# Turning the output projection and both feed-forward stages of a hybrid attention layer so that features lie on the partitions

## The chip, the cores and the metric

One core of a Trainium2 chip runs the whole layer in one program. Its engines have their own instruction streams: PE (matrix products, with PEld loading the stationary operand), DVE and POOL (both elementwise; POOL is GpSimd), ACT (activations, casts, copies), and SP, which issues most of the transfers (DMA). The metric is the device time of one execution in microseconds (us); less is better.

## The reference

The layer works on 1024 tokens with 1024 features, in float32:

```python
u = rms_norm(h, mix_norm_gain);  proj = u @ w_in
o_att = rms_norm(chunked_rel_attention(aq, ak, av, ...), att_out_gain)   # 8 heads of 64, band of 9 chunks
o_dn  = rms_norm(gated_delta_rule(dq, dk, dv, ...), dn_out_gain) * silu(dgate)   # 4 heads of 128
h = h + concat([o_att, o_dn]) @ w_out
z = rms_norm(h, ffn_norm_gain) @ w_ff1            # 1024 x 1024 by 1024 x 4096
h = h + square(relu(z)) @ w_ff2                   # 1024 x 4096 by 4096 x 1024
```

The change concerns the last three lines: the output projection with its residual, the norm behind it, and the two feed-forward products.

## The kernel before

**Arithmetic.** A float32 operand x is split into hi, which is x rounded to the type that PE multiplies fast (fp32r), and lo = x - hi. A product is then three matmuls: hi by hi, hi by lo, lo by hi. `split` (L130 to L137) does it with a cast on ACT (L134) and a subtraction on DVE or POOL (L137); names that end in `_h` and `_l`, or `h` and `l`, are such halves.

**Stages.** First the norm and all projections from u, then attention and the delta rule interleaved, then `out_proj` (PE tile `op`, L962 and following), `ff1` (tile `q`, L1095) and `ff2` (tile `p`, L1205). The order of the instructions on every engine is set by a scheduler that plans with a timeline of its own, under the limits that pools of buffers set: a tile gets a buffer only when the tile that held it has been read for the last time. No engine reorders at run time.

**Attention and delta rule.** Names with `t_` are one attention turn of 128 tokens (the last three of its steps: normalise the heads' outputs `t_on`, take them through POOL's reciprocal root `t_r`, transpose them into `t_tpo` on PE). Names with `c_` and `m_` are one chunk of the delta rule (`c_po` output, `c_o` its normalised form, `c_tpo` its transpose).

**Output projection.** Tokens lie on the partitions. For each half j of the output columns and each block t of 128 tokens, 24 matmuls multiply the block of mixer outputs with the weights `wo`; DVE adds the residual (L977) into `h`. When a block's both halves are done, its row norm follows: squares on ACT and DVE (L175), root on POOL, scaling (L182), and 8 transposes on PE (`v_tp`, L195; 64 in all), since ff1 wants features on the partitions. DVE and ACT write the transposed blocks with the gain into `b11`, `b21` (first 512 tokens) and `b12`, `b22` (last 512). The norm of the last two blocks is put behind the first two products of ff1 (`rest`).

**ff1.** A Strassen-Winograd scheme with 7 products instead of 8: the columns of w_ff1 are taken in 8 blocks of 512, and each block has products q1, q2, q5, q6, q3, q7, q4 of 24 matmuls each (1344 in all). The operands on the side of u (`b11`, `t1` to `t4`, ...) are made once; the weight sums `ws` are made in every block. Every second lo goes to POOL, the others to DVE; results go to the scratch tensor `f_dr`.

**ff2.** The same scheme over 4 groups of the inner dimension, 7 products of 48 matmuls in each (again 1344). Here both operands of every product are split anew, 512 columns at a time; every third lo goes to POOL, and POOL makes some of the sums (L1276, L1285, L1294). DVE adds the products into the accumulators (L1266); residual pages `r` come back from `h_dr`. In the very last product the matmuls are ordered by output bank ("turned"), so that the four banks end one after another.

All tiles are pages of 512 columns out of pools shared by all stages; PSUM is divided into four pools of 3, 2, 1 and 2 banks.

## Time and profile before

| | us |
|---|---|
| median of 3 runs (lowest, highest) | 1326.9 (1321.51, 1328.15) |
| the profiled execution: own time | 1324.08 |
| the profiled execution: span from first to last instruction | 1322.4 |
| PE busy in it | 1271.4 |
| DVE, POOL, ACT busy in it | 973.2, 717.3, 538.6 |

Rows of the profile are read like this. A row of groups or of the timeline names engine, line and operation, then output <- inputs with shapes; in a group the three numbers behind "xN:" are the shortest, median and longest duration in ns, and first and last start in us. In the view of stretches each engine has its busy us and, in brackets, how many instructions began there; PEclk is the TensorE clock granted, as a share of full speed; then come the share of time the DMA engines were busy and GB/s. Consecutive matmuls overlap, so a matmul listed with 0.39 us can follow another after 0.23 us: PE's rate is read from counts or from starts, not from durations.

### The profile page before, as it was taken

The numbers are of one execution on the slowest core, as the hardware profiler recorded it, in microseconds if no ns is written. First come the engines' busy times: TensorE is split into PE (matmuls) and PEld (weight loads), VectorE is DVE, ScalarE is ACT, GpSimd is POOL, SyncE is SP. The second block draws the span as 40 slices with busy tenths as digits, with TensorE's granted clock in tenths as the row PEclk, the third lists the DMA queues.
The fourth block names the chain that finished last, engine by engine and source line by source line (L and its number), as shares of the span: only waits on it lengthen the run. The fifth ranks groups of instructions, "written<-read, shape, count | busy, mean of one in ns | idle before, by whom it ended". The sixth has DMA issues, their size and how long they took to land.

```text
span 1322.4 us, 19653 instructions
## 1 busy us (share of the span) xinstructions
PE 1271.4 (96%) x6718; PEld 1042.8 (79%) x6718; DVE 973.2 (74%) x1627; ACT 538.6 (41%) x1128; POOL 717.3 (54%) x826
## 2 busy tenths in 40 slices
PE   8999999999999899999988999999997999989997
PEld 6778878788888788888866788888876887867776
DVE  7899969554156567764789966545569799998799
ACT  7232222222266566643653333333314544434331
POOL 4426542543124454651487766554488395683885
PEclk9999999999999999999988999999998999999999
DMA  7214354666564432163403333333581523314002
GB/s 217 69 44 142 95 156 119 151 168 165 191 199 147 135 92 73 38 210 96 128 18 126 109 116 118 112 112 128 195 299 40 166 83 113 119 56 129 31 33 96
DMA packets 133861, 159.71 MB, mean 121 GB/s; under 512 B 25216, under 2 KB 74368, under 8 KB 133760
## 3 DMA queue, kind: packets, MB, share of 16 engines
q1 hardware_dynamic: 125056, 154.25, 37.5%
q10 hardware_dynamic: 8704, 4.20, 1.4%
q8 instruction: 53, 0.87, 0.3%
q14 instruction: 48, 0.39, 0.1%
HBM read 111.22 MB, written 47.19 MB: 120 GB/s over the span
## 4 chain that ended last, share of the span: by engine, by line
PE 62%; DVE 17%; issue 7%; POOL 6%; DMA 4%; ACT 2%; SPq 0%; DVEq 0%; POOLq 0%; ACTq 0%
PE q L1095 18%; PE p L1205 6%; PE op L155 6%; PE av_ps L155 3%; PE aq_ps L155 3%; PE t_o L893 3%; PE g_ps L155 3%; PE ak_ps L155 2%; PE dq_ps L155 2%; PE dv_ps L155 2%; DVE r L1266 1%; POOL b L1276 1%; DVE s L1280 1%; PE t_tpa L883 1%; PE t_tpb L872 1%
## 5 line engine op out<-in xcount | busy, mean ns | idle before, releaser
L1102 POOL TENSOR_TENSOR z<-z 128x512 f32<-128x512 f32 x32 | 42.9, 1341 | 54.0 <-ACT z L1101 39.0
L836 DVE CUSTOM_DVE_ANT_0 t_pb<-t_sb,biasn 128x256 f32<-128x256 f32 (+1 forms) x64 | 25.7, 403 | 54.5 <-PE t_sb L821 29.1
L155 PE MATMUL op<-wo_l,op_h 128*128 128x512 f32 x128 | 50.5, 394 | 0.0
L155 PE MATMUL op<-wo_h,op_h 128*128 128x512 f32 x128 | 49.7, 392 | 0.8 <-DVE h L977 0.8
L155 PE MATMUL op<-wo_h,op_l 128*128 128x512 f32 x128 | 50.1, 392 | 0.0
L1101 ACT ACTIVATE z<-z 128x512 f32<-128x512 f32 x32 | 20.3, 633 | 53.0 <-DVE z L1154 19.9
L1266 DVE TENSOR_TENSOR r<-r,p 128x512 f32<-128x512 f32 x64 | 40.6, 675 | 0.0
L851 ACT ACTIVATE t_pb<-t_pb,t_nm 128x256 f32<-128x256 f32 (+1 forms) x64 | 31.6, 494 | 21.3 <-DVE t_nm L845 12.3
L1122 POOL TENSOR_TENSOR wa<-wa,wa 128x512 f32<-128x512 f32 x16 | 25.5, 1595 | 23.0 <-DVE ws L1109 23.0
L1109 DVE TENSOR_TENSOR ws<-wa,wa 128x512 f32<-128x512 f32 x16 | 16.1, 1007 | 25.9 <-DMA wa<-in_w_ff_dram 25.8
L1276 POOL TENSOR_TENSOR b<-b,b 128x512 f32<-128x512 f32 x16 | 24.6, 1539 | 18.1 <-DVE p13b_l L137 8.7
L1280 DVE TENSOR_TENSOR s<-s,a 128x512 f32<-128x512 f32 x16 | 24.7, 1544 | 10.0 <-POOL p53a_l L137 6.2
L1114 DVE TENSOR_TENSOR ws<-ws,wa 128x512 f32<-128x512 f32 x16 | 18.1, 1132 | 18.0 <-POOL q_3a_l L137 6.2
L845 DVE CUSTOM_DVE_ANT_0 t_pa<-t_sa,biaso,t_nm 128x384 f32<-128x384 f32 (+2 forms) x48 | 26.3, 548 | 5.2 <-PE t_sa L821 2.9
L1294 POOL TENSOR_TENSOR b<-b,b 128x512 f32<-128x512 f32 x16 | 25.9, 1621 | 7.8 <-DVE p21b_l L137 2.5
L1285 POOL TENSOR_TENSOR b<-b,b 128x512 f32<-128x512 f32 x16 | 26.8, 1686 | 5.1 <-DVE p50b_l L137 1.9
L178 POOL TENSOR_TENSOR v_st<-v_ss 128x1 f32<-128x1 f32 x8 | 2.8, 347 | 48.7 <-DVE v_ss L175 48.7
L155 PEld LDWEIGHTS op<-wo_h,op_h 128*128 128x128 f32 x128 | 24.0, 188 | 6.0 <-ACT op_h L134 1.2
L1104 DVE SCALAR_TENSOR_TENSOR z<-z 128x512 f32<-128x512 f32 x32 | 28.6, 893 | 0.0
L893 PE MATMUL t_o<-t_ta,vt 128*64 128x128 f32 x240 | 27.8, 287 | 0.5 <-DVE t_ta L886 0.3
L1274 DVE TENSOR_TENSOR s<-a,a 128x512 f32<-128x512 f32 x16 | 13.1, 824 | 20.5 <-DMA a<-f_dr 15.5
L155 PEld LDWEIGHTS op<-wo_l,op_h 128*128 128x128 f32 x128 | 24.0, 188 | 4.9 <-issue 0.2
(1271 smaller groups left out, 4904.2 us busy)
## 6 DMA issues: line engine op xcount, KB each, us to landing
wa<-in_w_ff_dram SPq DMA_DIRECT2D x64, 256.0 KB
f_dr<-z SPq DMA_DIRECT2D x64, 256.0 KB
a<-f_dr SPq DMA_DIRECT2D x64, 256.0 KB
b<-in_w_ff_dram SPq DMA_DIRECT2D x64, 256.0 KB
t_q<-q_dr SPq DMA_DIRECT2D x32, 256.0 KB
xt<-in_x_t_dram SPq DMA_DIRECT2D x16, 256.0 KB
ks<-k_dr SPq DMA_DIRECT2D x16, 256.0 KB
wo_r<-in_w_out_dram SPq DMA_DIRECT2D x16, 256.0 KB
```

The source lines that it names most:

```text
L155: nc.tensor.matmul(ps, a, b, start=(i == 0), stop=(i == n - 1))
L845: nc.vector.tensor_tensor_reduce(sa[e][:, 0:wa], bk[:, 0:wa], old[g][i][:, 384 - wa:384], -1.0, nm[:, 4 + i:5 + i], ALU.add, ALU.min, nm[: ...
L851: nc.scalar.activation(sb[:, c], sb[:, c], AF.Exp, bias=m, scale=-1.0, accum_out=T["sums"][:, 4 + i:5 + i])
L893: nc.tensor.matmul(po[64 * e:64 * e + 64, pp * P:(pp + 1) * P], vt[k0 + j][:, 64 * h:64 * h + 64], (ta[e] if j < na else tb)[:, c:c + P], ...
L1095: nc.tensor.matmul(ps[q], l[:, s], r, start=(i + k + m == 0), stop=(i + k == 2 and m == 2))
L1102: nc.gpsimd.tensor_tensor(t, t, t, ALU.mult)
L1104: nc.vector.scalar_tensor_tensor(t, t, 0.0, t, ALU.max, ALU.mult)
L1205: nc.tensor.matmul(ps[q], l[:, s], r, start=(i == 0 and m == 0), stop=(i == NK - 1 and m == 2))
L1266: nc.vector.tensor_tensor(y[q], y[q], ps[q], op)
L1276: nc.gpsimd.tensor_tensor(b11[i], b12[i], b11[i], ALU.subtract)
L1280: nc.vector.tensor_tensor(s1[i], s1[i], a11[i], ALU.subtract)
L1285: nc.gpsimd.tensor_tensor(b11[i], b22[i], b11[i], ALU.subtract)
```

## The change

- The output projection computes its transpose: weights are the stationary operand, the mixer outputs (stored transposed, four blocks to a tile of 2048 columns) the moving one. `rows` makes a quarter h[j, hf] (512 features, 512 tokens) in four banks; the residual comes from the transposed input `x_t`.
- The norm needs a sum over features, which now lie on partitions: ACT squares, POOL adds the squares up (L955 of the new kernel), matmuls with a column of ones (`hcol`) and with a broadcast of the scales (`hrow`) make a row of factors, and DVE scales 16 pages (L965). The 64 transposes and the row norm are gone. The norm of the second half of the tokens, formerly behind the first products of ff1, now stands ahead of them.
- A pool `quarters` of six tiles of 2048 columns holds in turn k^T, half of u's lo parts, the mixer outputs and their normalised forms, the four quarters of h, and ff1's and ff2's results.
- The mixer's pools are closed after the output projection. ff1 and ff2 get pools of their own with pages of 1024 columns and PSUM in four tiles of 1024 columns. Elementwise operations are half as many and twice as wide. POOL keeps the lo parts of b21 and b22, one subtraction and four merges at the end; in ff1 the second half of relu(z)^2 is squared by ACT.
- ff2 multiplies the transposed weights with f, so results are transposed too, and the host returns a transposed view of the output. The last product is no longer turned.
- The raw input pages use 8 buffers in place of 16.

```diff
     def row_scales(squares, hf, name, col, row):      # was row_scales(hf); now also for the second norm
...
         if c % TPH == 0:
+            mix[c // TPH][1] = quarter(f"mixd{c // TPH}")
...
+            if t % TPH == 0:
+                mix[t // TPH][0] = quarter(f"mixa{t // TPH}")
...
     def out_proj():
+        order = (4, 5, 6, 7, 0, 1, 2, 3)
...
+        def rows(j, hf, acc):
+            R[j, hf] = r = quarter(f"h{j}{hf}")
+            for i in range(4):
...
+                mm3(ps, [((w[j][k][0][:, s], w[j][k][1][:, s]), parts[hf][k]) for k in order])
+                nc.vector.tensor_tensor(part(r, i), ps, xt, ALU.add)
+                if i == 0 and acc is None:
+                    acc = page("on", n + "_q")
+                    nc.scalar.activation(acc, part(r, i), AF.Square)
+                else:
+                    sq = page("raw", n + "_q", w=516)[:, 0:512]
+                    nc.scalar.activation(sq, part(r, i), AF.Square)
+                    nc.gpsimd.tensor_tensor(acc, acc, sq, ALU.add)
+            nc.sync.dma_start(out=h_dr[j, hf], in_=q4(r))
+            return acc
+        def norm(hf, acc, js):
+            row = page("pp", f"hr{hf}")
+            row_scales([acc], hf, "h", r_col[:, TPH * hf:TPH * hf + TPH], row)
+            for j in js:
+                for i in range(4):
+                    r = part(R[j, hf], i)
+                    nc.vector.scalar_tensor_tensor(r, r, fgain[:, 4 * j + i:4 * j + i + 1], row, ALU.mult, ALU.mult)
+        weights(0)
+        mixed(0)
+        acc = rows(0, 0, None)
+        weights(1)
+        acc = rows(1, 0, acc)
+        norm(0, acc, (0, 1))
+        mixed(1)
+        acc = rows(1, 1, None)
+        acc = rows(0, 1, acc)
+        norm(1, acc, (0, 1))
+        return dict(b11=R[0, 0], b21=R[1, 0], b12=R[0, 1], b22=R[1, 1])
...
     def ff1(R, psw, pools):
...
+                split(t, hi, lo, nc.scalar, nc.gpsimd if key in ("b21", "b22") else nc.vector)
...
+            z11 = wide(zz, 0) if zz is not None else page2("ut4", f"z11_{sb}")
...
+            z12 = wide(zz, 1) if zz is not None else page2("ut4", f"z12_{sb}")
...
         def product(name, prep):                       # ff2
+            ps = [psw.tile([P, 1024], F32, tag="bk", name=f"{name}{m}") for m in range(2)]
+            for i in range(2):
+                ab = []
+                for o, src in zip("ab", prep(i)):
+                    hi = page2("h" + t, f"{name}{o}{i}_h", F32R)
+                    lo = page2("l" + t, f"{name}{o}{i}_l", F32R)
+                    split(src, hi, lo, nc.scalar, nc.vector)
...
-    ff1(*out_proj())
-    ff2()
+    R = out_proj()
+    mixer.close()
+    ffn(R)
```

The order of the instructions moves at four places. The rows that follow are the order on one engine, with the line number of the respective kernel.

**PE at the end of attention.** Before: `t_on` and `t_tpo` are the last turns, `op` the output projection, `c_po` the delta rule.

```order
L155 MATMUL op_6683<-wo_7_h,op_h_6684 128x512
L155 MATMUL op_6720<-wo_7_h,op_h_6721 128x512
L913 MATMUL t_on<-ident,t_pb_6518 128x128 x2
L502 MATMUL t_tpo<-ident,t_on 128x128 x4
L155 MATMUL op_6683<-wo_7_l,op_h_6684 128x512
L155 MATMUL op_6683<-wo_7_h,op_l_6685 128x512
L155 MATMUL op_6683<-wo_0_h,op_h_6688 128x512
```

After:

```order
L852 MATMUL t_o<-t_tb_6560,vt_3775 64x128 x2
L852 MATMUL t_o<-t_tb_6560,vt_3778 64x128 x2
L874 MATMUL t_on<-ident,t_pb_6500 128x128 x2
L460 MATMUL t_tpo<-ident,t_on 128x128 x8
L167 MATMUL op_6700<-ml_6666,wo_4_h 128x512
L167 MATMUL op_6700<-mh_6665,wo_4_l 128x512
L167 MATMUL op_6700<-mh_6669,wo_5_h 128x512
```

Before, 35 matmuls of the output projection (and a chunk's `c_po`) stand between the last turn's `t_on` and its transposes; now none does, and the transposes of the last two turns stand together. Only three `op` matmuls stand ahead of this place.

**DVE, first attention turns.** After, the rows that free the banks of the first two turns' transposes (`mixa<-t_tpo`, in one row) stand behind the fifth chunk's `mixd`; before, the corresponding L928 of the first two turns stood each in its turn's place, ahead of the fourth chunk's L717.

```order
L606 TENSOR_TENSOR c_jv<-c_tpv,br 128x512
L481 TENSOR_REDUCE c5q_ss<-c_tpq 128x4
L612 SCALAR_TENSOR_TENSOR c_jv<-c_pk,nbr,c_jv 128x128 x4
L676 SCALAR_TENSOR_TENSOR mixd_5069<-c_tpo,dng,c_jg 128x4x128
L891 TENSOR_TENSOR mixa_5825<-t_tpo,again 128x4x128 x2
```

Two banks (`ps_t`) serve the transposes of attention, so both are held until then.

**DVE from the last output bank to the first products of ff1**, after (`hcol` comes from PE, `hr` from ACT):

```order
L948 TENSOR_TENSOR h_7181<-op_7277,op_x 128x512
L129 TENSOR_SCALAR h_v<-hcol_7308 128x4
L134 TENSOR_TENSOR h_t<-h_y 128x4
L136 SCALAR_TENSOR_TENSOR h_t<-h_t,h_v 128x4
L137 SCALAR_TENSOR_TENSOR r_col<-h_t,h_y 128x4
L965 SCALAR_TENSOR_TENSOR h_7181<-h_7181,fgain,hr_7307 128x512 x4
L965 SCALAR_TENSOR_TENSOR h_7056<-h_7056,fgain,hr_7307 128x512 x4
L149 TENSOR_TENSOR b11l_7362<-h_6697,b11h_7361 128x1024
L1013 TENSOR_TENSOR h_6697<-h_7181,h_6697 128x1024
L1013 TENSOR_TENSOR h_7181<-h_7056,h_7181 128x1024
L149 TENSOR_TENSOR b11l_7366<-h_6697,b11h_7365 128x1024
L149 TENSOR_TENSOR q_0a_l<-wa_0_7351,q_0a_h 128x1024
```

PE has no other matmul between the norm's `hrow` and ff1's first product. Before, the splits of `b11` and `b21` stood ahead of the last two blocks' norms.

**SP at the end of ff1**, after:

```order
L1055 DMA f_dr<-zz_9144 128x2x512 x2
L1114 DMA y_9325<-h_dr 128x1024 x2
L1055 DMA f_dr<-yy_9084 128x2x512
L1055 DMA f_dr<-z_1_7819 128x2x512
L1151 DMA a_0_9339<-in_w_ff_dram 128x2x512
L1151 DMA a_0_9341<-in_w_ff_dram 128x2x512
L1151 DMA b_0_9343<-f_dr 128x2x512
L1151 DMA b_0_9345<-f_dr 128x2x512
```

`z_1_7819` is the page z12 of ff1's block 1; it takes a buffer of the tag `ut4`, which an operand of the last product of block 7 holds until that product ends. Its store now stands ahead of every load of ff2. Before, ff2's first loads stood among the last stores of ff1.

More of the change, by code (lines that the diff above doesn't have):

```diff
@@ L906, in finish @@
             if not g:
-                outs[t] = page("at", n + "_on")
+                if t % TPH == 0:
+                    on = quarter(n + "_on")
+                    outs.update((t + i, part(on, i)) for i in range(TPH))
             o = outs[t]
@@ L1229, in ff2, with store @@
+        def store(x, j, hf):
+            for m in range(2):
+                nc.sync.dma_start(out=out[0, (4 * j + 2 * m) * P:(4 * j + 2 * m + 2) * P, hf * TH:(hf + 1) * TH].rearrange(
+                    "(q p) t -> p q t", p=P), in_=two(x[m]))
         nb = DFF // (2 * NK * P)
```

632 lines of the change are left out of this document (255 added, 377 removed).

## The prediction

> **What bounds the kernel now.** I read the page first, for who is busy.
>
> ```profile
> PE 1271.4 (96%) x6718; PEld 1042.8 (79%) x6718; DVE 973.2 (74%) x1627; ACT 538.6 (41%) x1128; POOL 717.3 (54%) x826
> PE 62%; DVE 17%; issue 7%; POOL 6%; DMA 4%; ACT 2%; SPq 0%; DVEq 0%; POOLq 0%; ACTq 0%
> ```
>
> PE is the bound, and the chain that ended last runs through it; DVE's 17% and POOL's 6% of that chain are what an edit of the elementwise work can reach. Where they lie is told by the view of stretches around the two feed-forward stages.
>
> ```profile
> core 0: us, PE busy (x) PEld busy (x) DVE busy (x) ACT busy (x) POOL busy (x), PEclk, DMA share, GB/s
> 655.00:670.00 15.00, 14.79 (x73) 11.94 (x72) 9.34 (x19) 7.46 (x16) 9.52 (x15) 1.00 0.20 66
> 670.00:700.00 30.00, 22.35 (x87) 17.10 (x85) 27.62 (x32) 15.62 (x34) 26.48 (x13) 0.88 0.13 39
> 700.00:740.00 40.00, 38.16 (x153) 30.65 (x154) 39.01 (x43) 15.63 (x28) 28.86 (x21) 0.92 0.37 124
> 740.00:780.00 40.00, 40.00 (x178) 33.00 (x177) 25.69 (x32) 13.42 (x24) 28.00 (x20) 1.00 0.36 117
> 940.00:970.00 30.00, 30.00 (x134) 24.82 (x133) 13.52 (x20) 10.73 (x19) 17.84 (x14) 1.00 0.92 325
> 980.00:1010.00 30.00, 24.90 (x96) 19.32 (x95) 24.88 (x22) 11.29 (x21) 21.93 (x15) 0.89 0.35 121
> 1010.00:1050.00 40.00, 37.41 (x165) 30.30 (x164) 35.72 (x42) 17.81 (x32) 21.45 (x15) 1.00 0.39 124
> 1050.00:1100.00 50.00, 49.58 (x218) 40.53 (x217) 45.18 (x42) 21.87 (x40) 41.07 (x26) 1.00 0.23 75
> 1100.00:1150.00 50.00, 49.49 (x218) 40.33 (x217) 46.28 (x58) 21.29 (x38) 27.41 (x18) 1.00 0.45 148
> 1150.00:1200.00 50.00, 46.34 (x195) 35.68 (x194) 42.14 (x43) 18.28 (x33) 37.51 (x26) 1.00 0.20 63
> 1200.00:1250.00 50.00, 46.61 (x204) 37.90 (x204) 41.08 (x51) 19.43 (x34) 30.55 (x20) 1.00 0.26 85
> 1250.00:1300.00 50.00, 46.60 (x199) 36.56 (x198) 48.82 (x51) 18.26 (x33) 43.86 (x28) 1.00 0.07 27
> 1300.00:1316.00 16.00, 14.27 (x63) 11.47 (x62) 16.00 (x20) 1.14 (x2) 7.09 (x5) 1.00 0.26 99
> ```
>
> Busy PE is not yet PE at its rate, so I count matmuls. The timeline of PE in ff2 has these two rows, 63 matmuls apart:
>
> ```profile
> 1200.05 0.39 PE L1205 MATMUL p<-p62b_h,p62a_h 128*128 128x512 f32 x1
> 1214.33 0.39 PE L1205 MATMUL p<-p72b_h,p72a_h 128*128 128x512 f32 x1
> ```
>
> 14.28/63 = 0.2267 us each. At this rate three places lose time. From 655 to 740, 313 instructions began, 24 of them transposes (of 0.11 us, below): 289 x 0.2267 + 2.6 = 68 of 85 us, a loss of 17. From 980 to 1050: 261 x 0.2267 = 59 of 70, a loss of 11. From 1050 to 1316: 1097 x 0.2267 = 248.7 of 266, a loss of 17. ff1 itself, from 740 on, is full. The waits of PE by releaser name the cause: the first two rows are from 655 to 740, the others from 1100 to 1317.
>
> ```profile
> PE q L1095 <- POOL t1l L137: 4.2, 1, 4.2
> PE q L1095 <- DVE b22l L137: 4.0, 1, 4.0
> PE p L1205 <- DVE p33b_l L137: 2.4, 1, 2.4
> PE p L1205 <- POOL p53b_l L137: 2.3, 1, 2.3
> ```
>
> It is the lo parts that come late, on DVE and on POOL alike. Why they do is in the operations' durations:
>
> ```profile
> L1266 DVE TENSOR_TENSOR r<-r,p 128x512 f32<-128x512 f32 x64 | 40.6, 675 | 0.0
> L1280 DVE TENSOR_TENSOR s<-s,a x16: 677/1763/1796, 998.2 to 1252.6; 128x512 f32<-128x512 f32 x16
> L137 POOL TENSOR_TENSOR wo_l<-wo_r,wo_h x8: 1269/1294/1742, 557.1 to 581.4; 128x512 fp32r<-128x512 f32 x8
> L580 DVE COPY ad<-xd x1: 1121/1121/1121, 236.8 to 236.8; 128x1024 f32<-128x1024 f32 x1
> ```
>
> The same DVE operation takes 0.68 or 1.76 us, and POOL's 1.27 or 1.74; L1266, which reads PSUM, is always 0.675. Two SBUF inputs on DVE and a POOL operation at the same time hold each other up.
>
> **The change, part by part.** The sum is made against the profiled execution's own 1324.1 us.
>
> *1. ff2 without POOL: -13.* A group of the inner dimension has 336 matmuls, 336 x 0.2267 = 76.2 us. On DVE it now has 58 operations of 1024 columns (28 lo, 16 sums, 14 accumulations). None stands in the trace but the copy of 1.121 us, the lower bound; the upper one is twice L1266, 1.35. That is 65 to 78 us, with nothing to disturb it. I take 1.15, since a second operation of the same width pays its fixed part once: 67 us, 88% of PE's time, with splits about two products ahead. The loss falls from 17 to 4 (seams between the groups), and to 12 if DVE needs 1.35: a gain of 13, between 5 and 16.
>
> [...]
>
> *2. Transposes: -7.* The row that counts them, and a row of four transposes of the same size on PE:
>
> ```profile
> L195 PE MATMUL v_tp<-ident,v x64: 270/273/276, 621.7 to 676.4; 128*128 128x128 f32 x64
> 573.43 0.60 PE L502 MATMUL t_tpo<-ident,t_on 128*128 128x128 f32 x4
> ```
>
> Four take 0.60, the last of them 0.27, so the starts are 0.11 apart: 64 x 0.11 = 7. Sums and factors by matmul come instead (8 `hcol`, 8 `hrow`): +1.
>
> *3. The tail of attention: +9.* The chain from the last turn's `t_on` to its transposes in the timeline:
>
> ```profile
> 563.91 0.38 PE L913 MATMUL t_on<-ident,t_pb 128*128 128x128 f32 x2
> 570.84 1.49 DVE L921 TENSOR_SCALAR t_on<-t_on,t_r 128x512 f32<-128x512 f32 x1 [0.36 <-POOL t_r L129]
> ```
>
> From 564.3 to 572.3 (the end of L921) it takes 8 us, then the transposes of step 2's row follow, at 573.43; 35 matmuls stand between (35 x 0.2267 = 7.9). In the new order nothing does. POOL no longer has `wo_l` splits, which took a place in the chain and made L921 take 1.49; that may take 1.5 off. In the old order 18 more `op` matmuls (4 us) filled gaps just ahead of `t_on`; now three do, of which I count 2 us; and the first `op` waits for one more lo, 0.7. So 8 - 1.5 + 2 + 0.7 = 9, between 5 and 12. The matmuls themselves are not lost, they run later; PE's idle time is.
>
> *4. The first turns: +4.* Both banks for attention's transposes are held until the fifth chunk's output is done. Two ends of that chain, in the timeline of the same kind of step:
>
> ```profile
> 500.99 1.06 PE L498 MATMUL c_po<-c_vn,c_att 128*128 128x128 f32 x8
> 507.61 1.04 POOL L707 TENSOR_TENSOR c_o<-c_o,c_r 128x512 f32<-128x512 f32 x1
> ```
>
> 7.7 us, then `c_tpo` (0.6) and DVE (0.7): 9, in which PE has only the delta rule's own steps: three more of `c_po`'s kind (3.2) and transposes and small products of about as much, an estimate of 6.5. That leaves 2.5; with the turns behind it on one bank for a while, I take 4, between 0 (attention had slack to give) and 7.
>
> *5. The second norm: +5.* Its chain in the first norm of the program, where the same rows exist:
>
> ```profile
> 36.68 0.15 DVE L117 TENSOR_SCALAR r_v<-rcol 128x4 f32<-128x4 f32 x1
> 36.91 1.03 POOL L119 TENSOR_TENSOR r_y<-r_v,mhalf 128x4 f32<-128x4 f32 x1 [0.70 <-DVE r_v L117]
> 38.58 1.16 PE L296 MATMUL rrow<-ident,r_col 128*128 128x128 f32 x8 [0.62 <-DVE r_col L125]
> 39.77 0.58 ACT L299 COPY rr<-rrow 128x512 f32<-128x512 f32 x1 [6.62 <-PE rrow L296]
> ```
>
> 3.7 us from sum to row. Ahead of it: L948 as L1266 0.7, a square on ACT as L299 0.6, POOL's sum as `wo_l` 1.3 to 1.7, and `hcol` as `rrow` without its end 0.9: 3.7. Behind it: eight scalings of 0.63 (5.0) and five operations of 1.15 (5.8) until the lo parts of the first product are there. PE waits 18 us, and then DVE has 18 more operations of 1.15 (21 us) for the four products of 5.4 us that can run (21.8): level, but for four wide lo parts on POOL in the same stretch that disturb some of them, +2. And PE starts again slowly, as it did at the start of the program:
>
> ```profile
> 8.32 0.63 PE L345 MATMUL dk_ps<-ul,wdk_h 128*128 128x512 f32 x1
> 8.75 0.63 PE L345 MATMUL dk_ps<-uh,wdk_l 128*128 128x512 f32 x1
> 10.33 0.40 PE L345 MATMUL dk_ps<-uh,wdk_l 128*128 128x512 f32 x1
> 10.56 1.07 PE L345 MATMUL dk_ps<-uh,wdk_h 128*128 128x512 f32 x4
> ```
>
> 0.43 us apart, and 0.23 only from 10.33 on: with ten matmuls at 0.2 us more, 2 us. 18 + 2 + 2 = 22 against the 17 of now: +5, between 0 and 12 (POOL's disturbance on all 18).
>
> [...]
>
> *6. From ff1 to ff2: +4.* Now loads run ahead: 325 GB/s from 940 to 970. In the new order the first four pages wait for the store of z12, which waits for ff1's last product. Two operations of DVE (2.3), then 2 MB at 325 GB/s (6.5) and one lo (1.2): PE stands 10 us, restarts slowly (2), and p5 waits for three more pages (6 x 0.5 MB behind the first four are in after 16 us, p1 ends after 21): 3. 15 against 11: +4, between -1 and +9.
>
> *7. At nothing.* ff1 in full swing: its 178 matmuls in 40 us cover 26 us of DVE and would cover all of POOL's 28 as well at 0.68 for 1.3; two of four PSUM tiles are held by block 1 from its start to the end, and two are enough while an accumulation (1.15) is shorter than a product (5.4). The half number of raw input pages: DVE has them free before PE asks. The last product, not turned, ends with the same accumulate and store, +-1.
>
> Sum: -13 - 7 + 1 + 9 + 4 + 5 + 4 = +3. That is 1327 on the scale of the profiled execution, whose 1324.1 lies 2.8 below the median of the runs shown; in steps 3 to 6 I gave PE nothing to do in the waits where single matmuls will fit, so I go 2 below: **1325 us, no change**. Changes of under 0.5% (6.6 us) are about what a measurement of this kernel cannot tell from none.
>
> **The rivals.** *A: the waits are shorter than their bounds say; faster.* If attention loses 5 + 0, the norm 0, the seam -1 and ff2 gains 16: -16 - 7 + 1 + 5 - 1 = -18, 1306. For it: DVE's 0.68 wherever POOL is quiet, and POOL leaves the chains of steps 3 and 5 alone. Against: PE's order has no filler at three places, whatever the speed. *B: the exposed chains decide; slower.* The mechanism is PE without other work between the last turn, the norm and ff2's first loads: at the upper ends of 3, 5 and 6: 12 + 12 + 9 + 4 - 13 - 7 + 1 = +18, 1342. It decides once these three waits together are over 24 us longer than now. For it: the three places have no other matmul in PE's order; against: each upper end needs every engine of its chain to be late. *C: DVE becomes the bound of ff2.* From 76.2/58 = 1.314 us an operation on, DVE sets the pace; at 1.35 it costs 8 of the 13: 1333. Only twice the narrow row speaks for it. *D: the change does not do what it says*, that is, what makes L1280 take 1.76 instead of 0.68 is ACT's casts or the transfers, not POOL: then DVE stays behind PE, nothing is gained in ff2, 1338. Against it: L1266 is undisturbed beside the same casts.
>
> **How the numbers follow.** No change as worked out, with its own range of 1319 to 1332: 0.35. A 0.34; B 0.18; C 0.06; D 0.07. C lies on the bound of 0.5% and is halved: faster by over 0.5% 0.34, within 0.38, slower 0.28. The range of 1304 to 1343 goes from A's time to B's, with a little beyond at either side, and leaves 2 in 10.
>
> **What would show it.** Step 1: DVE rows of 128x1024 at 1.12 to 1.22 in ff2, and PE at some 220 matmuls in 50 us. Steps 3 and 4: PE waits of 6 to 9 us for DVE at `t_tpo`, and a first `op` after it. Step 5: one wait of PE for DVE of over 15 us ahead of `q`, PEclk under 0.9. Step 6: a wait for DMA of about 10 us ahead of the first `p`. It is wrong if ff2 still loses over 8 us, or if the three waits together stay under 15.

## The result: 1.5% slower

The changed kernel takes 1345.57 us (median of 4 runs, 1343.37 to 1349.01) against 1326.13 us for the kernel before on the same chip: a ratio of 1.0154, 95% interval 1.0118 to 1.019. The prediction said 1325 us, with a range up to 1343. The profiled execution has a span of 1347.1 us, 24.7 more than before; the medians differ by 19.4.

The page of the changed kernel, its busy times and the engines of its chain:

```profile
PE 1272.1 (94%) x6686; PEld 1048.7 (78%) x6686; DVE 931.0 (69%) x1395; ACT 509.6 (38%) x870; POOL 310.8 (23%) x513
PE 75%; DVE 5%; DMA 3%; ACT 2%; issue 1%; POOL 1%; SPq 0%; DVEq 0%; ACTq 0%; POOLq 0%
```

The plan worked on paper: POOL lost more than half of its work, DVE fell from 17% to 5% of the chain. Yet PE is busy for the same time in a longer span. Where it stands is shown by the view of stretches of the changed kernel (columns as in the prediction):

```profile
500.00:545.00 45.00, 39.19 (x364) 33.73 (x363) 28.22 (x77) 22.03 (x60) 23.68 (x52) 1.00 0.24 71
570.00:600.00 30.00, 19.51 (x114) 14.13 (x111) 20.02 (x32) 16.09 (x36) 11.97 (x18) 0.77 0.31 98
670.00:700.00 30.00, 18.00 (x79) 14.88 (x77) 9.13 (x14) 4.60 (x7) 7.84 (x6) 0.78 0.50 157
700.00:740.00 40.00, 27.94 (x111) 22.45 (x112) 39.72 (x31) 17.93 (x19) 10.11 (x3) 0.78 0.04 14
740.00:780.00 40.00, 40.00 (x178) 33.12 (x178) 31.08 (x27) 16.15 (x16) 0.00 (x0) 1.00 0.38 125
1020.00:1050.00 30.00, 17.36 (x64) 13.34 (x65) 19.95 (x18) 16.96 (x18) 3.81 (x2) 0.83 1.04 373
1050.00:1100.00 50.00, 50.00 (x223) 41.40 (x222) 46.70 (x42) 20.73 (x21) 0.00 (x0) 1.00 0.65 216
```

From 1050 on PE starts 223 matmuls in 50 us, its full rate (50/0.2267 = 220.6): ff2 loses nothing any more behind its start. But there are holes at 500 to 545, 570 to 600, 670 to 740 and 1020 to 1050, and in all of them but the first the granted clock is down to 0.77 to 0.83 as well. The waits of PE that belong to them:

```profile
PE q L1046 <- ACT q_0a_h L146: 10.8, 1, 10.8
PE q L1046 <- DVE q_0a_l L149: 8.3, 1, 8.3
PE t_tpo L460 <- DVE t_on L882: 6.9, 1, 6.9
PE c_po L456 <- POOL c_att L656: 2.0, 1, 2.0
PE p L1135 <- ACT p10b_h L146: 10.2, 1, 10.2
```

**Four stages.** Every profiled run has four marks in PE's timeline: the first transposes of attention's outputs (`t_tpo`), the last `op` matmul, the first `p` matmul, and the end. Their starts are 479.97, 683.70 and 1029.93 in the changed kernel, and 1347.1 is its end; the stages between them separate the places of the change. The last two columns are the median of the timed runs and the ratio to the kernel before on the same chip.

| run | A: to first `t_tpo` | B: to last `op` | C: to first `p` | D: to the end | median | ratio |
|---|---|---|---|---|---|---|
| before | 471.6 | 182.7 | 325.8 | 342.3 | 1326.1 | 1 |
| after | 480.0 | 203.7 | 346.2 | 317.2 | 1345.6 | 1.0154 |
| e1_lo_on_dve | 474.5 | 205.7 | 339.4 | 319.4 | 1341.4 | 1.0109 |
| e2_in_place | 474.9 | 190.5 | 347.1 | 316.0 | 1329.4 | 1.0023 |
| e3_filler_at_tail | 479.6 | 194.1 | 344.8 | 318.1 | 1335.5 | 1.0072 |
| e4_norm_behind_q1 | 473.6 | 203.5 | 346.6 | 316.8 | 1348.4 | 1.0155 |
| e5_z12_own_page | 479.1 | 203.7 | 344.9 | 315.9 | 1344.2 | 1.0126 |
| e6_pool_lo_in_ff2 | 479.5 | 204.3 | 344.6 | 321.8 | 1351.1 | 1.0175 |
| e7_before_dve_ff2 | 474.2 | 182.9 | 325.6 | 315.3 | 1299.3 | 0.979 |
| e8_five_edits | 475.5 | 182.5 | 339.4 | 314.4 | 1315.4 | 0.9903 |
| e9_last_stores_on_act | 478.2 | 206.3 | 341.8 | 315.5 | 1341.5 | 1.0108 |
| e10_b11_early | 473.7 | 212.2 | 357.7 | 316.1 | 1361.7 | 1.0274 |
| e11_seven_edits | 471.5 | 188.9 | 352.1 | 317.6 | 1334.6 | 1.0067 |
| e12_before_dve_ff | 476.4 | 183.1 | 325.2 | 315.5 | 1298.4 | 0.9802 |

Against before, the change is +8.4 in A, +21.0 in B, +20.5 in C and -25.1 in D: +24.8. Most of A is scatter between executions. Eleven profiled runs with the changed program take 471.5 to 480.0 there (mean 476.4), three with the old one 471.6 to 476.4 (mean 474.1), although no edit aims at A. The two means differ by 2.3; the other 6 of the 8.4 are scatter of these two executions: the changed one lies 3.6 above its mean, the old one 2.5 below its own. This fits the medians, which differ by 5 less than the profiled runs do. The other stages scatter less: in the runs of the changed program whose edit aims elsewhere, B lies between 203.5 and 206.3, C between 344.6 and 347.1, D between 316.0 and 319.4. A difference of 3 us in one of these stages thus shows nothing by itself. The rows of the stretch that scatters, first in the changed kernel, then in e4_norm_behind_q1:

```profile
448.00:456.00 8.00, 5.85 (x41) 4.75 (x41) 1.01 (x5) 1.56 (x4) 0.80 (x1) 0.70 0.46 148
464.00:472.00 8.00, 6.68 (x52) 5.20 (x50) 2.48 (x7) 3.04 (x9) 2.92 (x10) 0.76 0.47 104
```

```profile
448.00:456.00 8.00, 7.38 (x59) 6.17 (x60) 2.17 (x11) 2.43 (x7) 0.00 (x0) 0.79 0.38 112
464.00:472.00 8.00, 8.00 (x94) 6.65 (x93) 4.02 (x10) 4.06 (x11) 3.82 (x14) 1.00 0.08 16
```

The place is the same, a wait for attention's q; in the one execution the clock falls twice, in the other once.

### The profile page after: what moved, and what is told of

It is laid out like the page before. It is cut to its first block, busy times and chain, and to the rows that moved or that the text cites. A ratio compares the mean times of both kernels' runs of the same rounds, so it can differ in the third digit from the quotient of the medians.

```text
span 1347.1 us, 18016 instructions
## 1 busy us (share of the span) xinstructions
PE 1272.1 (94%) x6686; PEld 1048.7 (78%) x6686; DVE 931.0 (69%) x1395; ACT 509.6 (38%) x870; POOL 310.8 (23%) x513
## 4 chain that ended last, share of the span: by engine, by line
PE 75%; DVE 5%; DMA 3%; ACT 2%; issue 1%; POOL 1%; SPq 0%; DVEq 0%; ACTq 0%; POOLq 0%
PE q L1046 22%; PE p L1135 21%; PE op L167 7%; PE av_ps L167 3%; PE aq_ps L167 3%; PE t_o L852 3%; PE g_ps L167 3%; PE ak_ps L167 2%; PE t_tpb L831 1%; PE t_tpa L842 1%; DMA a<-in_w_ff_dram 1%; DMA t_q<-q_dr 1%; PE t_sb L779 1%; PE t_sa L779 1%; PE t_sb L780 1%
## 5 line engine op out<-in xcount | busy, mean ns | idle before, releaser
L1173 DVE TENSOR_TENSOR y<-y,p 128x1024 f32<-128x1024 f32 x50 | 60.3, 1220 | 7.6 <-PE p L1135 6.5
L167 PE MATMUL op<-ml,wo_h 128*128 128x512 f32 x128 | 51.6, 404 | 1.0 <-DVE ml L149 1.0
L167 PE MATMUL op<-mh,wo_h 128*128 128x512 f32 x128 | 51.2, 401 | 0.5 <-DVE t_nm L795 0.3
L167 PE MATMUL op<-mh,wo_l 128*128 128x512 f32 x128 | 51.3, 400 | 0.0
L955 POOL TENSOR_TENSOR op_q<-op_q 128x512 f32<-128x512 f32 x14 | 18.2, 1298 | 57.6 <-ACT op_q L954 57.6
L167 PEld LDWEIGHTS op<-ml,wo_h 128*128 128x128 f32 x128 | 24.7, 193 | 6.8 <-DVE ml L149 1.4
L167 PEld LDWEIGHTS op<-mh,wo_h 128*128 128x128 f32 x128 | 24.8, 193 | 6.6 <-DVE t_nm L795 0.6
L167 PEld LDWEIGHTS op<-mh,wo_l 128*128 128x128 f32 x128 | 24.8, 193 | 5.4
L813 ACT ACTIVATE t_pa<-t_pa,t_nm 128x384 f32<-128x384 f32 (+2 forms) x48 | 26.4, 551 | 0.1
L167 PE MATMUL g_ps<-uh,wg_l 128*128 128x512 f32 x64 | 25.3, 398 | 0.5 <-POOL wg_l L149 0.5
L167 PE MATMUL dq_ps<-uh,wdq_h 128*128 128x512 f32 x64 | 25.4, 397 | 0.0
```

The lines of the kernel that those rows point to most:

```text
L167: nc.tensor.matmul(ps, a, b, start=(i == 0), stop=(i == n - 1))
L813: nc.scalar.activation(sa[e][:, 0:wa], sa[e][:, 0:wa], AF.Exp, bias=m, scale=-1.0, accum_out=T["sums"][:, i:i + 1])
L955: nc.gpsimd.tensor_tensor(acc, acc, sq, ALU.add)
L1173: nc.vector.tensor_tensor(y[i][m], y[i][m], ps[m], op)
```

## The experiments

Theory: the change gains in ff2 because POOL is gone there, and loses more at four exposed places. General rival: the places are connected, so that a hole that is closed opens again further on.

### The start of ff1: POOL's last wide operations

```diff
-                split(t, hi, lo, nc.scalar, nc.gpsimd if key in ("b21", "b22") else nc.vector)
+                split(t, hi, lo, nc.scalar, nc.vector)
```

> The changed kernel with one edit: ff1 makes the lo parts of b21 and b22 on DVE instead of POOL, so POOL has no wide operation while DVE prepares the first products behind the second norm. Theory (POOL and DVE hold each other up in wide operations): the five wide DVE operations between the last scaling and the first q matmul, 12.2 us in the changed kernel at up to 3.4 each, go back to about 1.2 each, 6 in all; at most one of the four added lo parts stands ahead of the first product (+1.2). The first full product of ff1 comes 5 to 7 us earlier, and the time falls by 5 to 8 us, to about 1.010 of the kernel before. Rival (the operations are slow for another reason, the casts of ACT or the weights arriving at the same time): they stay over 2.5 us each, and four more operations on DVE make it 3 to 5 us slower, about 1.019.

The timeline of the changed kernel, DVE and then POOL, behind the second norm:

```profile
693.60 7.47 DVE L965 SCALAR_TENSOR_TENSOR h<-h,fgain,hr 128x512 f32<-128x512 f32 x8 [2.85 <-ACT hr L256]
702.24 6.56 DVE L1013 TENSOR_TENSOR h<-h,h 128x1024 f32<-128x1024 f32 x2
708.72 3.37 DVE L149 TENSOR_TENSOR b11l<-h,b11h 128x1024 fp32r<-128x1024 f32 x1
```

```profile
695.53 2.34 POOL L149 TENSOR_TENSOR b21l<-h,b21h 128x1024 fp32r<-128x1024 f32 x1 [5.37 <-ACT b21h L146]
700.90 3.52 POOL L149 TENSOR_TENSOR b22l<-h,b22h 128x1024 fp32r<-128x1024 f32 x1 [3.03 <-ACT b22h L146]
704.39 3.33 POOL L149 TENSOR_TENSOR b21l<-h,b21h 128x1024 fp32r<-128x1024 f32 x1
707.68 3.33 POOL L149 TENSOR_TENSOR b22l<-h,b22h 128x1024 fp32r<-128x1024 f32 x1
```

And DVE in e1_lo_on_dve:

```profile
689.34 5.39 DVE L965 SCALAR_TENSOR_TENSOR h<-h,fgain,hr 128x512 f32<-128x512 f32 x8 [2.85 <-ACT hr L256]
694.64 1.22 DVE L149 TENSOR_TENSOR b11l<-h,b11h 128x1024 fp32r<-128x1024 f32 x1
696.91 1.22 DVE L1013 TENSOR_TENSOR h<-h,h 128x1024 f32<-128x1024 f32 x1
```

The same operation takes 3.3 us while POOL works and 1.22 when it does not (only the first `b11l`, begun together with POOL's first `b22l`, took 1.21, and POOL's 3.52); even the eight scalings fall from 7.47 to 5.39, for one of them took 2.83 beside POOL's first 2.34, the others 0.74. Both engines' operations then end one per 3.3 us, close to the sum of what each takes alone (1.22 in e1, and 2.34 for POOL's add of the same width at 1021.5 in the changed kernel, where DVE is idle: 3.56). So in these rows they hardly overlap, though a pair takes 3.3 and not quite the sum.

Stage C falls by 6.8, the time from 1.0154 to 1.0109 of before. The theory holds, with a gain inside its 5 to 8 by the stage and at its lower edge by the medians (1.0154 - 1.0109 of 1326 = 6.0).

### The first turns of attention

```diff
+                    mix[t // TPH][0] = on
...
-            if t % TPH == 0:
-                mix[t // TPH][0] = quarter(f"mixa{t // TPH}")
-            nc.vector.tensor_tensor(q4(mix[t // TPH][0])[:, :, (t % TPH) * P:(t % TPH + 1) * P], b4(tp),
-                                    bc_row(again), ALU.mult)
+            nc.vector.tensor_tensor(b4(o), b4(tp), bc_row(again), ALU.mult)
```

> The changed kernel with one edit: attention's transposed outputs go back into the quarter that holds its normalised outputs, as in the kernel before, and no quarter of their own is taken; the split of the output projection reads them through a strided view. In the order, the writes of the first two turns then stand in their turns' places, not behind the fifth chunk's. Theory (two banks held until a quarter comes free stop PE between 500 and 545): the gaps at 502 to 516 us vanish and PE is busy for over 44 of the 45 us from 500 to 545, against 39.2; the last t_on starts some 5 us earlier and the time falls by 4 to 7 us, to about 1.011. Rival (the pause comes from attention's chain itself or from the delta rule, and the place of the writes is only where the planner had room): the gaps stay, less than 2 us move.

The DVE rows that free the two banks in the changed kernel; then the first such write in e2_in_place, and its stretch:

```profile
516.11 0.75 DVE L676 SCALAR_TENSOR_TENSOR mixd<-c_tpo,dng,c_jg 128x512 f32<-128x512 f32 x1 [0.93 <-PE c_tpo L460]
516.77 1.28 DVE L891 TENSOR_TENSOR mixa<-t_tpo,again 128x512 f32<-128x512 f32 x2
```

```profile
475.77 0.69 DVE L890 TENSOR_TENSOR t_on<-t_tpo,again 128x512 f32<-128x512 f32 x1
```

```profile
500.00:545.00 45.00, 44.98 (x432) 39.37 (x430) 31.42 (x94) 30.23 (x85) 20.82 (x56) 1.00 0.19 57
```

In the changed kernel both writes stand together behind the fifth chunk's `mixd` and come at 516.8; in e2 each comes in its turn, the first two at 475.8 and 489.3, and PE is full from 500 to 545 (44.98 against 39.19 us). So the pause was the missing quarter and the two banks held by it. Stage B falls by 13.2, about twice what was expected, and the median by 17 (1.0154 - 1.0023 of 1326) instead of 4 to 7. The place was right, the price missed: 26 `op` matmuls now also stand between the last `t_on` and its transposes, where the changed kernel has none (the quarter saved is probably the one that lets the output projection begin earlier; that was not tried apart). PE has a new wait there, of 6.0 us at `op` for a lo part of the mixer outputs. The time is 1.0023 (1.0006 to 1.004) of before.

### The tail of attention

```diff
-                                 (("wh", "u"), ("u", "wl"))[j])
+                                 (("wh", "u"), ("u", "u"))[j])
...
-                lo = page("u", f"ml{hf}{k}", F32R)
+                lo = page("wl", f"ml{hf}{k}", F32R)
```

> The changed kernel with one edit of tags: the lo parts of the mixer outputs take the tag wl, and both halves of the second weight pages the tag u. In the order, some 18 matmuls of the output projection then stand between the steps of the last attention turns. Theory (PE waits at attention's tail because no other work stands there, and its clock falls to half behind the wait): the wait for t_on of 6.9 us shrinks to under 3, the window from 570 to 600 us holds 27 or more of 30 us of busy PE against 19.5, and the time falls by 6 to 11 us, to about 1.009. Rival (the same matmuls are only moved, and the output projection ends when its DVE and ACT work ends): the last op matmul comes less than 3 us earlier, and the time falls by under 3 us.

The stretch of the tail in e3:

```profile
570.00:600.00 30.00, 26.95 (x173) 20.84 (x172) 17.74 (x36) 14.62 (x35) 11.13 (x18) 1.00 0.31 98
```

173 PE instructions against 114 in the same stretch, at a clock of 1.00 against 0.77; the wait at `t_tpo` is gone from the list of waits. Stage B falls by 9.6, more than the wait of 6.9: the half clock behind the wait (0.50 from 586 to 596 in the changed kernel) is in the price. In the window's busy time it is a hair under the expected 27, in the time (1.0072) inside the range. Both edits together (in e8_five_edits, below) take 21.2 off stage B, to 182.5 against the 182.7 of before: the two edits close all that the change opened there.

### The norm behind the first products

```diff
-        norm(1, acc, (0, 1))
+        c = r_col[:, TPH:2 * TPH]
+        row_scales([acc], 1, "h", c, None)
+        def rest(psw):
+            row = psw.tile([P, 1024], F32, tag="bk", name="hrow1")
...        (hrow and the eight scalings of b12, b22, called behind the first two products)
```

> The changed kernel with one part put back as it stood before: of the second norm only the column of scales is made ahead of ff1; the row of factors and the eight scalings of b12 and b22 stand behind the first two products of ff1, which need only b11, scaled by the first norm. Theory (PE waits for a chain of DVE, POOL and ACT that the first products do not need): from the last op matmul to the first product running through, 29.6 us in the changed kernel, falls to 8 to 16 us, bounded by the weights of the first products, whose loads start at 685 us and land by 700; the time falls by 12 to 18 us, to about 1.004. Rival (DVE has the same work in either order, and the products behind the first two wait for it as long as PE waited before): a wait of 10 us or more appears ahead of the third or fourth product, and the time falls by under 4 us.

PE's waits in e4 and its stretch from 700 to 740:

```profile
PE q L1061 <- DVE t1l L149: 5.5, 1, 5.5
PE q L1061 <- ACT t2h L146: 2.8, 1, 2.8
```

```profile
700.00:740.00 40.00, 30.29 (x114) 23.75 (x114) 35.76 (x33) 14.51 (x15) 9.11 (x2) 0.83 0.11 40
```

The first product runs through from 690.80, 13.7 us behind the last `op` (677.05), as expected for the wait itself. But stage C is 346.6 against 346.2, the time 1.0155 (1.0128 to 1.0183): nothing gained. After the two products PE waits for `t1l` and `t2h`, and starts 114 instructions from 700 to 740, against 111. The rival holds by the time, though its one wait of 10 us is here two of 5.5 and 2.8: the work of DVE is the same in either order, and PE waits for it sooner or later. The waits of 10.8 and 8.3 us were not worth what they showed.

### The start of ff2

```diff
-            z12 = wide(zz, 1) if zz is not None else page2("ut4", f"z12_{sb}")
+            z12 = wide(zz, 1) if zz is not None else wide(quarter("zz1"), 0) if sb else page2("ut4", f"z12_{sb}")
```

> The changed kernel with one edit: block 1's page z12 of ff1 gets half a quarter of its own instead of a buffer of tag ut4, which the last block's operand holds to the end of ff1. In the order, its store moves from the end of ff1 to the middle, and ff2's first loads stand ahead of ff1's last stores. Theory (ff2 starts late because its loads stand in the queue behind that store): PE's wait of 10.2 us ahead of the first p falls to under 4, the loads run while ff1's last products run, the stretch from the last op matmul to the first p falls from 346.2 to 336 to 340 us, and the time by 5 to 10 us, to about 1.009. Rival (the pages of ff2's first loads lie over pages that ff1's last products read, whatever the store does): the wait stays over 8 us and the time within 2 us.

The order changed as intended, yet PE's wait only went from 10.2 to 9.0, and C from 346.2 to 344.9, which is within the scatter: by the wait the rival holds, and the time is 1.0126 (1.0108 to 1.0143). SP's timeline of e5 tells why:

```profile
995.10 15.62 SPq L1055 DMA_DIRECT2D f_dr<-zz  x2
1017.85 0.36 SPq L1055 DMA_DIRECT2D f_dr<-yy  x1
1018.26 1.39 SPq L1151 DMA_DIRECT2D a<-in_w_ff_dram  x2
```

The loads now stand behind other stores of the last block: SP holds at `zz` for 15.6 us and then at `yy`, which starts at 1017.85, and the loads follow from 1018.26 on. That gave the next edit, on top of e5:

```diff
-                nc.sync.dma_start(out=f_dr[sb * 4 + fh * 2
+                (nc.scalar if sb == 7 else nc.sync).dma_start(out=f_dr[sb * 4 + fh * 2
```

> The kernel with z12's own page with one more edit: the four stores of ff1's last block are issued by ACT instead of SP, so in SP's order nothing that waits for the last block stands ahead of ff2's first loads. Theory (the loads are late because SP issues in order and its queue stands at stores whose data is not ready): the first loads of ff2 are issued 10 to 30 us earlier, PE's wait ahead of the first p falls from 9.0 to under 3 us, the stretch from the last op matmul to the first p from 344.9 to 334 to 338 us, and the time to about 1.006 of the kernel before. Rival (the loads wait for pages that the last products of ff1 read): they are issued after 1012 us as now, the wait stays over 7 us, and the time over 1.011.

SP in e9:

```profile
995.61 1.71 SPq L1151 DMA_DIRECT2D a<-in_w_ff_dram  x2
998.22 1.60 SPq L1151 DMA_DIRECT2D b<-f_dr  x2
1000.75 21.97 SPq L1151 DMA_DIRECT2D a<-in_w_ff_dram  x4
```

The first four loads go out 22 us earlier; then the queue holds again for 22 us, until ff1's last product has ended (1020). PE's wait is 5.9, C 341.8, the time 1.0108 (1.0071 to 1.0145; e5: 1.0126, the intervals overlap). The wait lies between what the two expectations had named, under 3 and over 7. What is left of it is not made by the loads that SP holds: the first product needs only the first four. ACT's timeline of e9 shows where their casts stand:

```profile
1022.80 1.06 ACT L1052 ACTIVATE yy<-yy 128x1024 f32<-128x1024 f32 x1
1024.30 1.04 ACT L146 CAST p10a_h<-a 128x1024 fp32r<-128x1024 f32 x1 [0.44 <-ACT yy L1052]
1025.25 1.04 ACT L146 CAST p10b_h<-b 128x1024 fp32r<-128x1024 f32 x1
```

ACT casts ff2's first operands only behind ff1's last squares (L1052), and the first `p` starts at 1026.34. So the order on SP held the first loads, and with these early the order on ACT holds the casts; an edit of ACT's order was not tried. SP's next loads are released, by the list of waits, when the last block's own stores have landed (`zz` 10.4 us and `yy` 7.1 at the longest); why they wait for these the rows do not tell.

### What won in ff2: width, or POOL's absence?

```diff
-            split(src, hi, lo, nc.scalar, nc.gpsimd if turn[0] % 3 == 0 else nc.vector)
+            split(src, hi, lo, nc.scalar, nc.vector)
...        (in the kernel before, ff2; its four kinds of subtraction on nc.gpsimd go to nc.vector too)
```

> The kernel before with one edit: in ff2 POOL's lo parts and its subtractions go to DVE; pages keep 512 columns and all else stays. A group then has 116 DVE operations of 0.675 us, 78 us against PE's 76.2. Theory (POOL's absence makes the win in ff2): all two-input DVE operations there take about 0.68 us, and the stretch from the first p to the end falls from 342 to 324 to 330 us; the time is 0.986 to 0.992 of the kernel before. Rival (the width makes the win; the narrow operations on DVE alone are too many): DVE is full, PE loses as much as before or more, and the time is between 0.997 and 1.01.

The kernel before, first and then with this edit, in groups of DVE from 1000 or 985 on, and a stretch with the edit:

```profile
L1280 DVE TENSOR_TENSOR s<-s,a 128x512 f32<-128x512 f32 x15 | 22.9, 1529 | 10.0 <-POOL p53a_l L137 6.2 <-POOL p52a_l L137 3.7
L1281 DVE TENSOR_TENSOR a<-a,s 128x512 f32<-128x512 f32 x16 | 20.4, 1276 | 1.8 <-POOL p23a_l L137 1.2 <-POOL p22a_l L137 0.6
```

```profile
L1280 DVE TENSOR_TENSOR s<-s,a 128x512 f32<-128x512 f32 x16 | 11.0, 686 | 0.0
L1281 DVE TENSOR_TENSOR a<-a,s 128x512 f32<-128x512 f32 x16 | 11.0, 686 | 0.0
```

```profile
1050.00:1100.00 50.00, 50.00 (x222) 41.44 (x221) 47.49 (x78) 22.98 (x41) 0.00 (x0) 1.00 0.27 83
```

1.53 and 1.28 us become 0.686, DVE does the whole of ff2 in 47.5 of 50 us, and PE is full. Stage D falls by 27.0, to 315.3, less than the changed kernel's 317.2; nothing else moves. The time is 1299.3 us, 0.979 (0.9769 to 0.9812) of before, below the theory's 0.986, since the start of ff2 speeds up too, which it had not counted: from 980 to 1050 PE starts 295 instructions instead of 261. So the pages of 1024 columns, the own pools and the transposition gave nothing in ff2 that five edited lines of the old kernel do not give.

The other direction, POOL back in the changed kernel:

```diff
-                    split(src, hi, lo, nc.scalar, nc.vector)
+                    turn[0] += 1
+                    split(src, hi, lo, nc.scalar, nc.gpsimd if turn[0] % 3 == 0 else nc.vector)
```

> The changed kernel with one edit: in ff2 every third lo part is made on POOL again, as in the kernel before, with the new pages of 1024 columns. DVE has less to do, POOL has work. Theory (the 25 us that ff2 won come from POOL's absence): DVE operations of 128x1024 that run beside POOL's take 2.5 to 3.4 us instead of 1.22, PE loses time again between the products, and the stretch from the first p to the end grows from 317 us by 10 to 25 us; the time is 1.023 to 1.034 of the kernel before. Rival (the win comes from half as many, wider operations and from pages that are free earlier): the stretch stays within 4 us of 317, the time within 1.013 to 1.018.

Groups of DVE in e6, and two stretches:

```profile
L1194 DVE TENSOR_TENSOR b<-b,b 128x1024 f32<-128x1024 f32 x8 | 16.9, 2111 | 0.0
L1199 DVE TENSOR_TENSOR b<-b,b 128x1024 f32<-128x1024 f32 x8 | 12.0, 1496 | 0.1
```

```profile
1050.00:1100.00 50.00, 47.30 (x202) 38.70 (x201) 49.90 (x34) 19.09 (x20) 15.82 (x6) 0.97 0.54 180
1150.00:1200.00 50.00, 50.00 (x222) 41.44 (x221) 41.82 (x32) 18.05 (x18) 16.21 (x7) 1.00 0.36 106
```

Here the theory missed, and the rival's numbers are met or nearly so: D is 4.6 longer (the rival: within 4), and 1.0175 (1.0147 to 1.0203) lies within its 1.013 to 1.018. DVE's operations are slowed (2.1 and 1.5 us), but PE is full from 1100 to 1300 and loses only at the start, with 202 instructions from 1050 to 1100 against 223. POOL is busy for 16 us in 50, where the kernel before had 27 to 44 in its rows from 1050 to 1300. So POOL still slows DVE here, and ff2 absorbs nearly all of it. Whether it does because POOL has a smaller share (the lo parts alone, without the subtractions of before), or because the wide pages leave more slack, was not tried apart. What is shown is e7's side: POOL's absence alone is enough for the whole gain.

### Together, and what did not help

> The changed kernel with the edits of five runs together: lo parts of b21 and b22 on DVE, attention's outputs written back in place, the tags that put output projection matmuls between the last turns, the norm's second half behind the first two products of ff1, and z12 with a page of its own. Theory (five separate places, each with its own price): from the changed kernel's 1345.6, -13 for the writes in place, -7 for the lo parts, -8 for z12, 0 to -4 for more filler at the tail, which the writes in place have half closed, and 0 to -6 for the norm, which gained nothing while POOL slowed DVE down: 1308 to 1318, 0.987 to 0.994 of the kernel before. Rival (the edits close the same gaps, and a wait that one removes comes back at the next place): 1322 to 1330, 0.997 to 1.003.

e8 combines e1 to e5's edits: 1315.4 us, 0.9903 (0.9886 to 0.992), inside the theory's 1308 to 1318, but partly by luck. B is back to 182.5, 21.2 less where the theory had 13 to 17. C is 339.4, what e1 alone reached: z12's page, priced at 8, brought nothing, and the norm's place is worth nothing without POOL either. A is 4.5 shorter by its scatter. So in B the two edits nearly add up (13.2 and 9.6 alone), and in C the rival of connected places holds but for POOL's part. DVE then works from 664.6 to 711 with 1.4 us of gap, wide operations at 1.22 each, and PE waits.

```diff
+        b11 = quarter("b11h", F32R), quarter("b11l", F32R)
+        for i in range(2):
+            split(wide(R[0, 0], i), wide(b11[0], i), wide(b11[1], i), nc.scalar, nc.vector)
         acc = rows(1, 1, None)
...
-            yy = quarter(f"yy{sb}")
-            y1, y5 = wide(yy, 0), wide(yy, 1)
+            y1, y5 = (page2("ub11", f"yy{i}_{sb}") for i in (1, 5))
```

> The changed kernel with the lo parts of b21 and b22 on DVE, and one more edit: the halves of b11 go into two of the six quarters, which are free by then, so that they are made during the last eight banks of the output projection, when DVE is busy for a third of the time; ff1's results y take the pages that b11 had. Theory (what is left of the slow start is DVE's work that the closing of the mixer's pools holds back): two DVE operations and two casts leave the start, the stretch from the last op matmul to the first p falls from 339.4 to 336 to 338 us, the time by 1 to 4 us, to about 1.009. Rival (the first product waits for the weights and the norm, not for b11): less than 1 us.

A clear miss: 1.0274 (1.0246 to 1.0302), 22 us worse than e1. Two waits of PE in e10:

```profile
PE p L1137 <- ACT p10b_h L146: 25.5, 1, 25.5
PE op L167 <- DVE h L948: 5.5, 1, 5.5
```

From the last `op` to the last `q` it takes 331.7 against 329.4 in e1, so the early halves gained nothing at the start of ff1. They cost 5.5 us in the output projection, and 25.5 ahead of ff2, where y now lies in pages that had been free early. I read that as the price of memory taken from those two places; it was not tried apart. The trace shows only that ff2's first cast waits 16.9 us for its load, while the share of the transfers is at 0.99 to 1.05 from 1025 on.

> The kernel of five edits with the last two as well: b11 split early into quarters, and the last block's stores on ACT. Theory (separate places): from its 1315.4, -8 to -10 at ff2's start and -1 to -3 at ff1's: 1302 to 1307, 0.982 to 0.986 of the kernel before; that is still above the kernel before with ff2's elementwise work on DVE (0.979). Rival (the gains overlap with those already in): over 1311, above 0.988.

e11, e8 with the edits of e9 and e10, is 1334.6 against the 1302 to 1307 of its theory: e10's loss outweighs e9's gain (18.9 us of waiting ahead of the first `p`). The last run asks whether the lesson of ff2 holds in ff1 of the kernel before:

```diff
-            split(src, hi, lo, nc.scalar, nc.gpsimd if turn[0] % 2 else nc.vector)
+            split(src, hi, lo, nc.scalar, nc.vector)
...        (ff1's weight operands, on top of e7's edit)
```

> The kernel before with ff2's elementwise work on DVE and one more edit: ff1's lo parts of the weight operands, every second of which POOL made, are on DVE too (the lo parts on the side of u stay as they are). Theory (POOL beside DVE costs more than it carries): in the steady part of ff1 DVE is busy for about 37 of 40 us and PE stays full at 178 matmuls; at the start, where PE lost 17 us in the kernel before, the lo parts come sooner, and the stretch from the last op matmul to the first p falls from 325 to 319 to 324 us; the time is 0.974 to 0.979 of the kernel before. Rival (DVE is short at the start of ff1 whoever slows it, and POOL's share there helps): the stretch grows to 328 to 335 us, the time to 0.982 to 0.988.

0.9802 (0.9778 to 0.9825) against e7's 0.979, C 325.2 against 325.6: neither. From 670 to 700 PE starts 119 instructions instead of 98 (e7), from 700 to 740 128 instead of 141: the hole at the start of ff1 moves and stays as large, and in full swing PE was full with POOL as well. Taking POOL's work away pays where PE waited for it, not everywhere.

## Why the prediction was wrong, step by step

The mechanisms that it named are there, and so are most of its signs (PE's 6.9 us for DVE at `t_tpo`, 0.78 of the clock ahead of ff1, 10.2 us ahead of the first `p`). What failed are the sizes of steps 3, 4 and 5. Put on the four stages, the prediction's steps are: A 0; B +9 (steps 3 and 4, +13, less 40 of the 64 transposes, 4.5, and half of the new small matmuls); C +13 (step 5, +5, the other 24 transposes, and the 10 us of step 6 that stand ahead of the first `p`); D -19 (step 1, -13, and step 6's 11 of now against 5). Measured: +8.4, +21.0, +20.5, -25.1.

- **Step 1, ff2 without POOL (-13).** The mechanism is right. DVE's 128x1024 operations take 1.22 us, at the upper end of the 1.12 to 1.22 named (1.12 was the copy; no row of the kernel before shows 1.22 at this width); PE starts 223 in 50 us. The loss of 17 is gone, not 4 left: -17, one beyond the step's end. Rivals C and D fall with it.
- **Step 2, transposes (-7).** Not tried apart.
- **Steps 3 and 4, attention's tail and first turns (+13): the first that failed.** They cost 21 to 25, more than their two upper ends together (12 + 7): e8, which undoes both, takes 21.2 off, and B's 21.0 with the 4 us of transposes that it no longer holds is 25. The places were right (the banks held until the fifth chunk, no filler at the last turn, PE's wait of 6.9 for DVE at `t_tpo`). The sizes were not. Step 4 subtracted 6.5 us of the delta rule's work as cover and let attention catch up; in the trace PE lost 5.8 of 45 us there. Step 3 priced the wait alone, without a slower clock behind it (0.77 from 570 to 600).
- **Step 5, the second norm (+5): the second.** From the last `op` (683.70) to 740 PE starts 111 products, 25.2 us of work, and 2 of `hcol` and `hrow` at the full clock: a loss of 29, +12 against the 17 of now. Step 5 had "+2" for POOL's four wide lo parts; they cost 6.8 (e1). Without them the loss is 22, against the step's 20 without that term. It kept the price as the upper end of its range (12), having seen 0.68 turn into 1.76 for narrow operations, and did not ask what 1.15 would turn into beside an operation of twice the width.
- **Step 6, ff1 to ff2 (+4).** Right in size: from 1019.5 to 1050 PE starts 64 matmuls, 14.5 us of 30.5, a loss of 16 against 11. The reason was wrong in the main: with z12's store out of the way 9.0 of the 10.2 us remain (e5), since other stores of the last block hold the loads on SP and ff1's last squares hold the casts on ACT (e9).
- **Step 7.** Right: 178 matmuls in 40 us from 740 on.
- **Stage A (0).** No step spoke of it. Of its 8.4, some 6 are the scatter of two executions.
- **The reduction of 2** for matmuls that would fit into the waits pointed the wrong way: the waits brought the half clock with them (0.50 from 586 to 596, 688 to 716 and 1026 to 1034).

Rival B, "the exposed chains decide", 1342 us with a chance of 0.18, is what happened. Its condition was three waits over 24 us longer than now; tail, norm and ff2's start came to 9.6, 12 and 5 (27), the first turns to the rest. For the slower clock behind a wait the prediction's sum has 2 us for each of two restarts, read from the slow start of the program. The rows show 0.77 to 0.83 in four stretches of 30 or 40 us, 5 to 9 us each in clock alone, part of it time in which PE would have stood anyway; the kernel before had 0.88 to 0.92 in its three such rows.

## What to carry to other kernels

When POOL and DVE share the elementwise work, read the shortest and the longest duration of the same DVE operation first; where they differ as here (0.68 and 1.76 us), try giving all of it to DVE alone before any rebuilding. Here that edit of five lines brings 2.1%, and the rebuilding, for the same gain in ff2, lost more at its seams. Asking for one tile more (e2), and probably closing and reopening pools, moves work to places where PE has no other; price such a place with the wait, the slower clock behind it, and with every operation of another engine that runs beside the chain. And a long wait is no proof of a gain: where the engine behind it is full, as in e4 (DVE busy for 35.8 of the 40 us from 700 on), moving the wait away moves nothing.

## What the runs showed of the hardware that I had not expected

- Beside a POOL operation of 2.34 us a DVE operation of 1.22 took 3.3, three times of four from 701 to 712, and POOL's took 3.3 to 3.5: over this stretch DVE was slowed 2.7 times, as much as narrow operations at the worst (0.68 to 1.76, 2.6 times; 1.28 to 1.53 in the mean of two groups).
- The clock fell to half after a wait of PE of only 1.3 us. The changed kernel's timeline and its stretches around it, PE alone:

```profile
467.04 0.36 PE L779 MATMUL t_sb<-ks,t_q 128*128 128x256 f32 x1 [1.27 <-DMA t_q<-q_dr]
```

```profile
469.00:470.00 1.00, 1.00 (x12) 0.50 0.00 0
476.00:478.00 2.00, 2.00 (x28) 1.00 0.00 0
```

It stays at half until about 475, with PE busy throughout, which costs PE some 3 us of work (half of 6.5); the wait before it, 17 us earlier, had been 3.1 us. In e4 the wait at the same place is 0.9 us, and there is no drop. A short wait for DMA thus cost more here than it shows; from which length on, these runs do not tell.
